# One PSUM pool, three column chunks by k half, and x through DRAM on ScalarE's queue, in a four-layer macaron trunk

## The chip, the cores and the metric

The kernel runs on one core of a Trainium2 chip. The metric is device time in microseconds (us) for one execution, lower is better; the time before is the median of three runs. TensorE is called PE, its weight loads PEld, VectorE DVE, ScalarE ACT, GpSimd POOL, and SyncE, which here only issues DMAs, SP. A name with a q (SPq, ACTq) is an engine's instruction queue.

## The reference

Four layers, each a sandwich of two half-weighted SwiGLU blocks around a mixer, on x of 256 rows by 1024 columns in float32:

```
for i in range(4):
    x = x + 0.5 * swiglu(rms_norm(x, norm_g[i, 0]), ffn_gate[i, 0], ffn_up[i, 0], ffn_down[i, 0])
    x = x + mixer_i(rms_norm(x, norm_g[i, 1]))      # i % 3: short conv, MLA, spatial gating
    x = x + 0.5 * swiglu(rms_norm(x, norm_g[i, 2]), ffn_gate[i, 1], ffn_up[i, 1], ffn_down[i, 1])

swiglu(x, g, u, d) = (silu(x @ g) * (x @ u)) @ d          # 1024 -> 2816 -> 1024
short conv:  b, c, h = split(x @ w_in, 3);  (b * causal_conv3(c * h)) @ w_out
MLA:         16-head latent attention, a = x @ w_a (416 columns), rotary parts, causal softmax
spatial:     u, v = split(gelu(x @ w_in), 2);  (u * (w_s @ rms_norm(v) + b_s)) @ w_out
```

All products are wanted at nearly float32 precision.

## The kernel before, in words

**Streams and turns.** The 256 rows are two streams of 128 rows, t0 and t1, and each runs the same twelve blocks (FFN, mixer, FFN, four times). A Python generator per stream writes the instructions in order by hand (every engine is in `MANUAL`), one *unit* of weights at a time. Turns alternate: t1, t0, t1, t0, and t0 is ahead by four advances (`LAG`). In a turn `advance` (L976) finishes the low parts of the weights made before, lets the stream write its next unit's matmuls, counts the turn and then runs the work that was put off with `later(n, ...)` and is now due (L170). So `later(1, ...)` is written at the end of the same turn, `later(8, ...)` at the end of the seventh turn after.

**Weights.** A unit is 128 x 1024 float32 values, two k tiles of 512 columns or one of 1024. SP loads it into one of six raw buffers (L91), ACT writes a rounded high part (L104), DVE the low part, the difference (L111). Each k tile of a 512-column product is three matmuls (L291, L292, L294): high x high, high x low, low x high. Both streams use the same unit, t1 four to five turns' worth of units later; there are nine buffers. A unit is made three units ahead of t0 (`AHEAD`, four counting its own), two ahead while a stream is between two blocks (`CHAIN_AHEAD`).

**Columns by k half.** A block starts with its input in two halves of 512 columns (four k tiles each), `lhs[t][0]` and `lhs[t][1]`. `linear_pair` (L344) runs the first two 512-column chunks of a block (gate and up of an FFN, c and h of the conv, both v of the spatial block) together: first half of k for both, then second half for both. That is four units of the stream, eight turns, before the second half is read. All other chunks take all eight k tiles in turn (`linear`, L296).

**x between two blocks.** A block ends in `rows_into_x` (L315), with the columns 0 to 511 of x done first, then 512 to 1023: four units later in an FFN, two in a mixer. After each half `prepare_x` (L400) turns it for the next block. By DMA: DVE transposes 32 x 32 blocks (L409); SP writes 256 KB to DRAM at the end of that turn (L414) and reads it back rearranged with four DMAs three turns later (L418); four turns after that ACT takes it with the gain (L423), writes the high part (L245), and DVE the low part (L246). By PE: four transposes (L253) into a PSUM tile, a DVE multiply by the gain (L433), then the same split. The DMA way is used after every FFN (`n % 3 != 1`, L968), PE after every mixer.

After its last unit a stream idles for two turns of its own (four ahead of MLA) in `normed` (L446), while the other goes on.

**Queues.** SP's queue is in program order and carries the raw loads (each waits for its buffer), the FFN's own way through DRAM (L267, L271) and x's writes and reads.

**PSUM.** Six banks are one pool for accumulators, `acc()`; two are another for transposes, `trp()`.

Of the kernel before, what the change touches and what calls it, by code (L numbers as in the profile page):

```python
# [13 lines left out]
F32 = mybir.dt.float32  # L14
# [33 lines left out]
N_ACC = 6  # L48
# [11 lines left out]
C_TURN, C_WAIT = 2, 0  # L60
WARM = (4, 6)
# [61 lines left out]
def trunk(ctx: ExitStack, tc: tile.TileContext, x, positions, norm_g, ffn_gate, ffn_up, ffn_down,  # L123
# [214 lines left out]
    def plan_pair(w0, w1, c0, c1, width, n_kt):  # L338
# [5 lines left out]
    def linear_pair(t, a, width, n_kt, first_done):  # L344
# [55 lines left out]
    def prepare_x(t, h, i, which, by_dma):  # L400
# [4 lines left out]
        if not by_dma:  # L405
            later(X_TURN, lambda: turn_by_pe(t, h, g))
            return
# [45 lines left out]
    def plan_ffn(i, j):  # L453
        for n, (c, w) in enumerate(FF_CHUNKS):
            if n == 0:
                plan_pair(ffn_gate[i, j], ffn_up[i, j], c, c, w, NK)
            else:
                W.add(ffn_gate[i, j], c, w, NK, UNIT // w)
                W.add(ffn_up[i, j], c, w, NK, UNIT // w)
        plan_rows(ffn_down[i, j], DFF // P, DOWN_TAIL)  # L460

    def ffn(t, i, j, _, then):
        a, r = yield from normed(t, IDLE_FIRST if i + j == 0 else (IDLE_DMA, IDLE_PE)[j])
        hs = []
        sg = [None]

        def gate_done(ps, w):
            sg[0] = slot([P, w])
            nc.scalar.activation(sg[0], ps[:, :w], AF.Silu, scale=r)  # L469

        for n, (c, w) in enumerate(FF_CHUNKS):
            if n == 0:
                up = yield from linear_pair(t, a, w, NK, lambda ps: gate_done(ps, w))
            else:
                gate = yield from linear(t, a, w, NK)
                gate_done(gate, w)
                yield
                up = yield from linear(t, a, w, NK)
            if n % 2 == 0:
                k0 = 0  # L480
                nk = sum(w for _, w in FF_CHUNKS[n : n + 2]) // P
                z = big([P, 4, nk, 32])
            h = slot([P, w])
            nc.vector.scalar_tensor_tensor(out=h, in0=up[:, :w], scalar=r, in1=sg[0], op0=ALU.mult, op1=ALU.mult)  # L484
            nc.vector.transpose(z[:, :, k0 : k0 + w // P].rearrange("p j k b -> p k j b"),  # L485
                                h.rearrange("p (k j b) -> p k j b", j=4, b=32))
            k0 += w // P
            if k0 == nk:
                turned(z, nk, hs)
            yield  # L490
# [3 lines left out]
    def plan_conv(ia):  # L494
        for j in range(2):
            if j == 0:
# [517 lines left out]
```

## Time and profile before

| | |
|---|---|
| median of 3 runs | 1893.94 us (1893.45 to 1894.00) |
| the profiled execution | 1896.66 us, its span 1894.9 us |
| mean granted TensorE clock | 0.994 |
| PE busy | 1851.4 us, 98% of the span, 8542 matmuls |
| DVE, ACT, POOL busy | 59%, 48%, 6% |
| DMA | 397 MB, 210 GB/s on average |

Busy shares are averages over the whole span. A matmul's listed duration contains the fill of the pipeline, so that consecutive matmuls overlap; the step from one start to the next tells what one costs. In brackets at the end of a timeline row stands how long the engine was idle before it and what ended that.

### The profile page before, as it was taken

To read this page: it belongs to the slowest core of one execution; us is meant where nothing else is said; L and a number is where in the kernel's file an instruction comes from. 1 tells how busy PE (TensorE), PEld (TensorE's weight loads), DVE (VectorE), ACT (ScalarE), POOL (GpSimd) and SP (SyncE) were. 2 spreads that over 40 slices of the span, in tenths; PEclk is the share of its full clock that TensorE was granted. 3 is DMA by queue.
4 is the path that set the end of the run, shared out by engine and by line. 5 is a ranking of instruction groups with operands and counts; after the bars stand their busy time and mean duration, and the time that the engine had idled before them with its cause. 6 is when DMAs were issued, how large, how long until landed. Compare 5 with 4: busy or idle time off the path is not lost.

```text
span 1894.9 us, 23349 instructions
## 1 busy us (share of the span) xinstructions
PE 1851.4 (98%) x8542; PEld 1512.8 (80%) x8542; DVE 1118.0 (59%) x1357; ACT 908.4 (48%) x1276; POOL 114.7 (6%) x222
## 2 busy tenths in 40 slices
PE   9999999999999969999989999999999999999999
PEld 7888788888788858888868887888887888788887
DVE  6565676564556466665556555666645664676563
ACT  5443554443544376544445445454445444545442
POOL 1000100000511031000010001000000000000000
PEclk9999999999999989999999999999999999999999
DMA  7776656786778640577757775567866776656782
GB/s 259 243 238 217 200 183 193 235 246 209 221 224 250 199 132 24 177 236 237 239 174 258 237 243 176 179 189 234 253 208 217 235 244 210 200 188 194 239 259 87
DMA packets 220563, 397.12 MB, mean 210 GB/s; under 512 B 16646, under 2 KB 74144, under 8 KB 220448
## 3 DMA queue, kind: packets, MB, share of 16 engines
q1 hardware_dynamic: 219440, 393.94, 66.0%
q0 software_dynamic: 608, 1.11, 0.3%
q8 instruction: 67, 1.10, 0.2%
q10 hardware_dynamic: 400, 0.57, 0.1%
q14 instruction: 48, 0.39, 0.1%
HBM read 364.10 MB, written 31.46 MB: 209 GB/s over the span
## 4 chain that ended last, share of the span: by engine, by line
PE 88%; DMA 4%; ACT 3%; DVE 3%; SPq 1%; issue 1%; ACTq 0%; DVEq 0%
PE acc L294 28%; PE acc L291 28%; PE acc L292 28%; DMA s<-xturn 3%; PE tr L253 2%; DVE wlo L111 1%; ACT s L423 1%; SPq L418 1%; ACT s L245 1%; DVE s L246 1%; DMA xturn<-s 1%; PE acc L919 1%; PE acc L892 1%; DVE x L394 0%; ACT whi L104 0%
## 5 line engine op out<-in xcount | busy, mean ns | idle before, releaser
L291 PE MATMUL acc<-whi,s 128*128 128x512 f32 (+1 forms) x2664 | 1029.8, 387 | 20.2 <-ACT s L245 19.3
L292 PE MATMUL acc<-wlo,s 128*128 128x512 f32 (+1 forms) x2664 | 1022.2, 384 | 1.5 <-DVE wlo L111 1.5
L294 PE MATMUL acc<-whi,s 128*128 128x512 f32 (+1 forms) x2664 | 982.0, 384 | 7.4 <-DVE s L246 7.3
L111 DVE TENSOR_TENSOR wlo<-raw,whi 128x1024 fp32r<-128x1024 f32 (+1 forms) x634 | 748.0, 1213 | 143.8 <-ACT whi L104 143.4
L104 ACT ACTIVATE whi<-raw 128x1024 fp32r<-128x1024 f32 (+1 forms) x634 | 635.7, 1048 | 158.0 <-PE acc L294 140.1
L291 PEld LDWEIGHTS acc<-whi,s 128*128 128x128 f32 x2664 | 502.6, 189 | 129.5 <-ACT s L245 26.1
L294 PEld LDWEIGHTS acc<-whi,s 128*128 128x128 f32 x2664 | 502.4, 189 | 119.1 <-DVE s L246 14.2
L292 PEld LDWEIGHTS acc<-wlo,s 128*128 128x128 f32 x2664 | 502.9, 189 | 105.0 <-DVE wlo L111 2.1
L469 ACT ACTIVATE s<-acc,rstd 128x512 f32<-128x512 f32 (+1 forms) x96 | 62.7, 654 | 460.7 <-PE acc L294 454.7
L484 DVE SCALAR_TENSOR_TENSOR s<-acc,rstd,s 128x512 f32<-128x512 f32 (+1 forms) x96 | 67.7, 705 | 207.4 <-PE acc L294 207.1
L278 DVE TENSOR_TENSOR s<-big,s 128x512 fp32r<-128x512 f32 x96 | 61.8, 644 | 128.8 <-ACT s L277 128.8
L246 DVE TENSOR_TENSOR s<-s,s 128x512 fp32r<-128x512 f32 (+1 forms) x58 | 39.6, 683 | 114.7 <-ACT s L245 114.7
L383 POOL TENSOR_TENSOR total<-ss,ss 128x1 f32<-128x1 f32 x26 | 14.1, 542 | 1449.5 <-ACT s L375 1449.5
L423 ACT ACTIVATE s<-s,columns 128x128 f32<-128x128 f32 x112 | 35.8, 390 | 94.0 <-DMA s<-xturn 94.0
L394 DVE SCALAR_TENSOR_TENSOR x<-acc,x 128x512 f32<-128x512 f32 x32 | 22.0, 689 | 98.8 <-PE acc L294 98.8
L375 ACT ACTIVATE s<-x 128x512 bf16<-128x512 f32 x48 | 30.0, 625 | 86.6 <-DVE x L394 50.1
L277 ACT ACTIVATE s<-big 128x512 fp32r<-128x512 f32 x96 | 56.2, 586 | 26.6 <-DMA big<-turn 26.6
L485 DVE STREAM_TRANSPOSE big<-s 128x512 f32<-128x512 f32 (+1 forms) x96 | 64.1, 668 | 3.3
L245 ACT ACTIVATE s<-s 128x512 fp32r<-128x512 f32 (+1 forms) x58 | 36.4, 627 | 46.7 <-DVE s L433 21.4
L253 PE MATMUL tr<-ident,s 128*128 128x128 f32 (+1 forms) x222 | 33.8, 282 | 7.6 <-ACT s L864 2.6
L253 PEld LDWEIGHTS tr<-ident,s 128*128 128x128 f32 (+1 forms) x222 | 26.4, 140 | 15.1 <-ACT s L864 4.4
L520 DVE SCALAR_TENSOR_TENSOR s<-s,columns,s 128x128 f32<-128x128 f32 x64 | 22.5, 352 | 2.3
(124 smaller groups left out, 432.2 us busy)
## 6 DMA issues: line engine op xcount, KB each, us to landing
raw<-in_ffn_gate_dram SPq DMA_DIRECT2D x176, 512.0 KB, 4.6
raw<-in_ffn_up_dram SPq DMA_DIRECT2D x176, 512.0 KB, 5.0
raw<-in_ffn_down_dram SPq DMA_DIRECT2D x176, 512.0 KB, 4.9
raw<-in_conv_w_in_dram SPq DMA_DIRECT2D x48, 512.0 KB, 4.4
turn<-big SPq DMA_DIRECT2D x32, 512.0 KB, 3.7
big<-turn SPq DMA_DIRECT2D x128, 128.0 KB, 4.7
raw<-in_conv_w_out_dram SPq DMA_DIRECT2D x16, 512.0 KB, 4.8
raw<-in_sg_w_in_dram SPq DMA_DIRECT2D x16, 512.0 KB, 4.6
```

Source lines behind the costliest of these rows:

```text
L104: nc.scalar.activation(hi, src, AF.Copy)
L111: self.nc.vector.tensor_tensor(out=lo, in0=src, in1=hi.bitcast(F32), op=ALU.subtract)
L246: nc.vector.tensor_tensor(out=lo, in0=src, in1=hi.bitcast(F32), op=ALU.subtract)
L253: nc.tensor.transpose(tr[: part.shape[-1], n, :], part, ident)
L277: nc.scalar.activation(hi.rearrange("p k (i b) -> p k i b", b=32), src, AF.Copy)
L278: nc.vector.tensor_tensor(out=lo.rearrange("p k (i b) -> p k i b", b=32), in0=src, in1=hi.bitcast(F32).rearrange("p k (i b) -> p k i b", b ...
L291: nc.tensor.matmul(ps, lhsT=ah[:, k, :], rhs=wh[:, wk, c], start=first, stop=False)
L292: nc.tensor.matmul(ps, lhsT=ah[:, k, :], rhs=wl[:, wk, c], start=False, stop=False)
L294: nc.tensor.matmul(ps, lhsT=al[:, k, :], rhs=wh[:, wk, c], start=False, stop=last)
L469: nc.scalar.activation(sg[0], ps[:, :w], AF.Silu, scale=r)
L484: nc.vector.scalar_tensor_tensor(out=h, in0=up[:, :w], scalar=r, in1=sg[0], op0=ALU.mult, op1=ALU.mult)
L485: nc.vector.transpose(z[:, :, k0 : k0 + w // P].rearrange("p j k b -> p k j b"), h.rearrange("p (k j b) -> p k j b", j=4, b=32))
```

## The change

PSUM becomes one pool of eight banks, `banks`, for both kinds of tile. `plan_pair` and `linear_pair` become `plan_group` and `linear_group`, which take any number of chunks, each with a function to call when its sum is complete; three chunks go by k half at the start of an FFN (gate 0, up 0, gate 1), of the conv (c, h, b of the first 512 columns) and of the spatial block (both v, first u). The rest of those blocks is rewritten in the same order of chunks. In the spatial block the product of the first u with its mix is put off by four turns (`U_WAIT`). The write of x to DRAM and its four reads go to ACT's queue. And which half goes by DMA is chosen per half: after an FFN both, but ahead of MLA only the first (the second by PE); after a mixer the second by DMA (before, both by PE).

```diff
+U_WAIT = (4, 0)
...
-    ps_acc = ctx.enter_context(tc.tile_pool(name="ps_acc", bufs=N_ACC, space=PSUM))
-    ps_tr = ctx.enter_context(tc.tile_pool(name="ps_tr", bufs=8 - N_ACC, space=PSUM))
+    banks = ctx.enter_context(tc.tile_pool(name="banks", bufs=8, space=PSUM))
...
-        return ps_acc.tile([P, 512], F32, tag="acc", name=name("acc"))
+        return banks.tile([P, 512], F32, tag="bank", name=name("acc"))
...
-        return ps_tr.tile([P, 4, P], F32, tag="tr", name=name("tr"))
+        return banks.tile([P, 4, P], F32, tag="bank", name=name("tr"))
...
+    def plan_group(parts, width, n_kt):
         for k in range(0, n_kt, n_kt // 2):
-            W.add(w0, c0, width, k + n_kt // 2, UNIT // width, k)
-            W.add(w1, c1, width, k + n_kt // 2, UNIT // width, k)
+            for w, c0 in parts:
+                W.add(w, c0, width, k + n_kt // 2, UNIT // width, k)
...
+    def linear_group(t, a, width, n_kt, done):
-        ps = [acc(), acc()]
+        ps = [acc() for _ in done]
         for k0 in range(0, n_kt, n_kt // 2):
-            for n in range(2):
+            for n in range(len(done)):
                 k = k0
                 while k < k0 + n_kt // 2:
                     w = unit(t)
                     for j in range(w[2]):
                         products([ps[n][:, :width]], a[(k + j) // 4], (k + j) % 4, w, j, [slice(0, width)], k + j == 0, k + j == n_kt - 1)
                     k += w[2]
-                    if k == n_kt and n == 0:
-                        first_done(ps[0])
-                    if k < n_kt or n == 0:
-                        yield
-        return ps[1]
+                    if k == n_kt:
+                        done[n](ps[n])
+                    yield
...
-    def prepare_x(t, h, i, which, by_dma):
+    def prepare_x(t, h, i, which, halves_by_dma):
...
-        if not by_dma:
+        if not halves_by_dma[h]:
             later(X_TURN, lambda: turn_by_pe(t, h, g))
             return
...
         def write():
-            nc.sync.dma_start(out=d.rearrange("i a j k b -> (i a) j k b"), in_=z)
+            nc.scalar.dma_start(out=d.rearrange("i a j k b -> (i a) j k b"), in_=z)
         def read():
             for j in range(4):
-                nc.sync.dma_start(out=y[32 * j : 32 * j + 32], in_=d[:, :, j].rearrange("i a k b -> a i k b"))
+                nc.scalar.dma_start(out=y[32 * j : 32 * j + 32], in_=d[:, :, j].rearrange("i a k b -> a i k b"))
...
     def plan_ffn(i, j):
+        gate, up = ffn_gate[i, j], ffn_up[i, j]
+        plan_group([(gate, 0), (up, 0), (gate, 512)], 512, NK)
+        W.add(up, 512, 512, NK, 2)
...
+        yield from linear_group(t, a, 512, NK, [lambda ps: gate_done(0, ps), lambda ps: up_done(0, ps), lambda ps: gate_done(1, ps)])
         for n, (c, w) in enumerate(FF_CHUNKS):
+            if n > 1:
+                gate_done(n, (yield from linear(t, a, w, NK)))
                 yield
+            if n > 0:
+                up_done(n, (yield from linear(t, a, w, NK)))
+                yield
...
+        yield from linear_group(t, a, 512, NK, [lambda ps, f=f: f(0, ps) for f in (c_done, h_done, b_done)])
+        for f in (c_done, h_done, b_done):
+            f(1, (yield from linear(t, a, 512, NK)))
             yield
...
+            later(U_WAIT[j], lambda: u_mixed(j))
...
+        yield from linear_group(t, a, 512, NK, [v_done, v_done, lambda ps: u_done(0, ps)])
...
-                then = (next_i, 2 * next_j, n % 3 != 1) if next_kind == "ffn" else (next_i, 1, True)
+                if next_kind == "ffn":
+                    then = (next_i, 2 * next_j, (n % 3 == 2, True))
+                else:
+                    then = (next_i, 1, (True, next_kind != "mla"))
```

## Rows read from the trace of the kernel before

**Rows 1.** The page, busy time of the engines (share of the span) xinstructions.

```profile
PE 1851.4 (98%) x8542; PEld 1512.8 (80%) x8542; DVE 1118.0 (59%) x1357; ACT 908.4 (48%) x1276; POOL 114.7 (6%) x222
```

**Rows 2.** Waits of PE: who waited for whom: us in total, times, longest us.

```profile
PE acc L291 <- ACT s L245: 19.3, 11, 7.1
PE acc L294 <- DVE s L246: 7.3, 6, 1.2
PE tr L253 <- ACT s L864: 2.6, 2, 2.1
```

**Rows 3.** Timeline of PE at the first FFN's end, and one later row.

```profile
202.98 0.39 PE L294 MATMUL acc<-whi,s 128*128 128x512 f32 x1
204.57 0.50 PE L291 MATMUL acc<-whi,s 128*128 128x512 f32 x1 [1.20 <-ACT s L245]
...
208.35 0.50 PE L294 MATMUL acc<-whi,s 128*128 128x512 f32 x1 [1.21 <-DVE s L246]
208.69 0.39 PE L291 MATMUL acc<-whi,s 128*128 128x512 f32 x1
...
1616.32 0.50 PE L291 MATMUL acc<-whi,s 128*128 128x512 f32 x1 [0.37 <-ACT s L245]
```

**Rows 4.** Timeline of PE at the start of t1's second half in FFN five.

```profile
989.96 0.80 PE L291 MATMUL acc<-whi,s 128*128 128x512 f32 x1 [2.80 <-ACT s L245]
...
993.48 0.40 PE L294 MATMUL acc<-whi,s 128*128 128x512 f32 x1
```

**Rows 5.** Timeline of PE at the start of the MLA block.

```profile
677.75 0.71 PE L291 MATMUL acc<-whi,s 128*128 128x416 f32 x1 [7.08 <-ACT s L245]
...
683.04 0.35 PE L291 MATMUL acc<-whi,s 128*128 128x416 f32 x1
...
685.49 0.46 PE L291 MATMUL acc<-whi,s 128*128 128x416 f32 x1 [0.26 <-ACT s L245]
```

**Rows 6.** Windows: length, busy of PE, PEld, DVE, ACT, POOL, PEclk, DMA share, GB/s.

```profile
677.50:683.00 5.50, 5.25 (x15) 4.68 (x16) 3.18 (x4) 4.00 (x7) 0.94 (x3) 0.52 0.30 97
990.00:994.00 4.00, 4.00 (x11) 3.17 (x12) 3.96 (x5) 2.75 (x3) 1.01 (x3) 0.57 0.72 229
```

**Rows 7.** Timeline of ACT at the first FFN's end.

```profile
192.00 1.31 ACT L423 ACTIVATE s<-s,columns 128x128 f32<-128x128 f32 x4 [6.56 <-DMA s<-xturn]
...
202.58 1.28 ACT L423 ACTIVATE s<-s,columns 128x128 f32<-128x128 f32 x4 [4.53 <-DMA s<-xturn]
```

**Rows 8.** Timeline of SP's queue there; merged rows run to the last issue's end.

```profile
192.36 4.06 SPq L414 DMA_DIRECT2D xturn<-s  x2
...
197.66 3.97 SPq L418 DMA_DIRECT2D s<-xturn  x8
```

**Rows 9.** One line each: issues of x's reads (ns min/median/max), their landing.

```profile
L418 SPq DMA_DIRECT2D s<-xturn x112: 302/423/1170, 185.3 to 1624.2; - x112
...
DMA to landing us min/median/max: 1.8/3.4/6.7
```

**Rows 10.** The same for x's writes.

```profile
L414 SPq DMA_DIRECT2D xturn<-s x28: 337/345/345, 182.6 to 1619.5; - x28
...
DMA to landing us min/median/max: 2.0/2.1/5.4
```

**Rows 11.** The page, DMA issues on ACT's queue: xcount, KB, us to landing.

```profile
s<-in_norm_g_dram ACTq DMA_DIRECT2D x1, 48.0 KB, 3.4
```

**Rows 12.** Timeline of PE around the four transposes of one half of x.

```profile
283.92 0.60 PE L253 MATMUL tr<-ident,x 128*128 128x128 f32 x4
...
284.59 0.39 PE L292 MATMUL acc<-wlo,s 128*128 128x512 f32 x1
284.82 0.40 PE L294 MATMUL acc<-whi,s 128*128 128x512 f32 x1
```

**Rows 13.** Timeline of DVE (first) and PE (second) after the second block boundary.

```profile
490.82 3.50 DVE L111 TENSOR_TENSOR wlo<-raw,whi 128x1024 fp32r<-128x1024 f32 x3 [0.41 <-ACT whi L104]
...
493.13 0.40 PE L292 MATMUL acc<-wlo,s 128*128 128x512 f32 x1
```

More of the change, by code (lines that the diff above doesn't have):

```diff
@@ L47 @@
 N_DRAM = 4
-N_ACC = 6
 AHEAD = 4
@@ L453, in plan_ffn @@
     def plan_ffn(i, j):
[L454 to L459, printed above, removed]
+        gate, up = ffn_gate[i, j], ffn_up[i, j]
+        plan_group([(gate, 0), (up, 0), (gate, 512)], 512, NK)
+        W.add(up, 512, 512, NK, 2)
+        for c, w in FF_CHUNKS[2:]:
+            for m in (gate, up):
+                W.add(m, c, w, NK, UNIT // w)
         plan_rows(ffn_down[i, j], DFF // P, DOWN_TAIL)
@@ L464, in ffn @@
         hs = []
[L465 to L469, printed above, removed]
-        for n, (c, w) in enumerate(FF_CHUNKS):
[L472 to L476, printed above, removed]
-                yield
[L478 to L490, printed above, removed]
+        sg = [None] * len(FF_CHUNKS)
@@ new lines, in ffn, with gate_done, up_done @@
+        z = []
+        def gate_done(n, ps):
+            w = FF_CHUNKS[n][1]
+            sg[n] = slot([P, w])
+            nc.scalar.activation(sg[n], ps[:, :w], AF.Silu, scale=r)
+        def up_done(n, ps):
+            w = FF_CHUNKS[n][1]
+            nk = sum(w for _, w in FF_CHUNKS[n - n % 2 : n - n % 2 + 2]) // P
+            if n % 2 == 0:
+                z[:] = [big([P, 4, nk, 32]), 0]
+            h = slot([P, w])
+            nc.vector.scalar_tensor_tensor(out=h, in0=ps[:, :w], scalar=r, in1=sg[n], op0=ALU.mult, op1=ALU.mult)
+            k0 = z[1]
+            nc.vector.transpose(z[0][:, :, k0 : k0 + w // P].rearrange("p j k b -> p k j b"),
+                                h.rearrange("p (k j b) -> p k j b", j=4, b=32))
+            z[1] += w // P
+            if z[1] == nk:
+                turned(z[0], nk, hs)
@@ L500, in plan_conv @@
+        for part in (1, 2, 0):
+            W.add(conv_w_in[ia], part * D + 512, 512, NK, 2)
         plan_rows(conv_w_out[ia], NK, OUT_TAIL)
@@ L590, in v_done @@
             sums.append(square_sum(vv))
-        v_done((yield from linear_pair(t, a, 512, NK, v_done)))
-        yield
-        rv = factor(sums)
+            if len(vs) == 2:
+                rv.append(factor(sums))
+                for j in range(2):
+                    later(3 + j, lambda j=j: normal(j))
+        rv = []
         mixed = [None] * 2
@@ L614, in gated, with u_done, u_mixed @@
             ms[j] = lhs_of(m, 4)
-        for j in range(2):
-            later(3 + j, lambda j=j: normal(j))
-        for j in range(2):
-            u = yield from linear(t, a, 512, NK)
-            us = slot([P, 512])
-            nc.scalar.activation(us, u, AF.Gelu_apprx_tanh, scale=r)
-            m = slot([P, 512])
-            nc.vector.tensor_tensor(out=m, in0=us, in1=mixed[j].rearrange("p k n -> p (k n)"), op=ALU.mult)
-            later(2, lambda j=j, m=m: gated(j, m))
-            yield
+        us = [None] * 2
+        def u_done(j, ps):
+            us[j] = slot([P, 512])
+            nc.scalar.activation(us[j], ps, AF.Gelu_apprx_tanh, scale=r)
+            later(U_WAIT[j], lambda: u_mixed(j))
+        def u_mixed(j):
+            m = slot([P, 512])
+            nc.vector.tensor_tensor(out=m, in0=us[j], in1=mixed[j].rearrange("p k n -> p (k n)"), op=ALU.mult)
+            later(2, lambda: gated(j, m))
+        yield from linear_group(t, a, 512, NK, [v_done, v_done, lambda ps: u_done(0, ps)])
+        u_done(1, (yield from linear(t, a, 512, NK)))
+        yield
         yield from rows_into_x(t, lambda k: ms[k // 4], NK, OUT_TAIL, 1.0, then)
```

40 lines of the change are left out of this document (14 added, 26 removed).

## The prediction, on record before the changed kernel was seen

> **What bounds the kernel now.** I read the page's busy shares first. The reader is to see that PE is the bound engine almost everywhere: 1851.4 of 1894.9 us, while ACT and DVE have 48% and 59% [rows 1]. Then the step between matmul starts: in an undisturbed stretch it is 0.23 us for 128x512 (284.59 to 284.82, [rows 12]), and nothing in this change alters the number or the form of those matmuls. So only time in which PE stands, runs at the lower clock level, or does transposes can be won. The view of PE's waits says how much there is to win and who is late: 19.3 us on ACT's L245 in 11 places and 7.3 us on DVE's L246 in 6 [rows 2]. L245 and L246 split x into high and low parts: PE waits for the normed input of the next block, at block boundaries after an FFN, and hardly anywhere else.
>
> The timeline of one such boundary shows two gaps [rows 3]: 1.20 us before t1's first unit (the high part of t1's first half is late) and 1.21 us before t0's fifth unit (the low part of t0's second half is late). From 202.98 to 208.69 there are ten starts, which at 0.23 us would take 2.3 us; they took 5.71. So the boundary costs 3.4 us, of which 2.4 is listed as idle and 1.0 lies in slow restarts. There are six boundaries of that kind (three FFN to FFN, three FFN to a mixer other than MLA), from 204.57 to 1616.32. Beside them stand two larger holes: 2.80 us in the fifth FFN before t1's second half [rows 4], and 7.08 us in MLA before t0's second half [rows 5].
>
> Why is x late? ACT, which takes it from DRAM, sits idle 6.56 and 4.53 us for the DMA [rows 7]. SP's queue shows the cause: t1's first half was ready to be written at 192.3 and was (192.36), but its reads were issued only at 197.66, because SP, in order, first held the write of t0's second half (which waits for DVE) and a raw load [rows 8]. The reads themselves then land after 3.4 us in the median, up to 6.7 [rows 9].
>
> **The change, part by part.** The sum is made against the profiled execution (span 1894.9, itself 1896.66); the median of the runs is 1893.94, and differences are carried over to it unchanged.
>
> (a) *Three chunks by k half.* The second half of x is first read after six of the stream's units instead of four. With both streams running that is four turns of six matmuls, 4 x 6 x 0.23 = 5.5 us later. It removes the second gap of all six boundaries (1.2 us, far under 5.5) and the 2.80 us hole of [rows 4]. After that hole PE also ran at a granted clock of 0.57 [rows 6], the 1.2 GHz level for most of it: from 989.96 to 993.48 eight steps took 3.52 us instead of 1.84: another 1.7 us. So 2.80 + 1.7 = 4.5 us. The first gap is not touched by this: t1's first half is needed when it was before, and it is what is late next.
>
> (b) *x on ACT's queue.* The write of t1's first half (ready at 192.3) goes out behind ACT's take of t0's first half and one squared sum, and lands 2.1 us later [rows 10], about 194.9. Its reads follow in ACT's order then, not at 197.66: four issues of 0.423 us [rows 9] end at 196.7, and with a landing time of 3.4 us the data is there at 200.1. ACT has by my count two whi of 1.05 us and the reads of t0's second half to pass before the take and reaches it at about 200.6; four copies and the split take 1.9 us, so the high part is ready near 202.5. PE would need it at 203.2, where it began to stand [rows 3]. The first gap closes with 0.7 us to spare. Together with (a) the six boundaries give back their 7.3 + 6.7 us of listed gaps (6.7 is the sum of the six waits on L245, 1.20 the first and 0.37 the last of them, [rows 3]) and 1.0 each of restarts: 14.0 + 5.9 = 19.9 us. Since the margin is thin, I leave 2 us of it in place.
>
> (c) *MLA: second half by PE.* PE stood 7.08 us before t0's second half and 0.26 before t1's [rows 5], and after the first it ran at a granted clock of 0.52 [rows 6]: 15 steps from 677.75 to 683.04 took 5.29 us where 0.19 us each (416 of 512 columns of 0.23) would make 2.85. By PE the half needs only residual, four transposes, a multiply and a split, and t0 is idle for four of its turns in between. So 7.34 + 2.4 = 9.7 us go. What is late next there is ACT, busy 4.0 of 5.5 us and more from there on; I count nothing inside MLA as won.
>
> (d) *Transposes on PE.* Four transposes and the slow restart take 284.59 - 283.92 = 0.67 us, where the one matmul in it costs 0.23: 0.44 us for a half [rows 12]. Eight halves (four mixers, two streams) leave PE, two (MLA) come: -6 x 0.44 = -2.6 us. The eight halves now by DMA after mixers are read 12 turns plus two idle ones after they are written to x, with the take due after eight; I cost that at nothing as long as the three chunks cover it. Without them it would be due as late as (a)'s.
>
> (e) *The price on ACT.* 34 halves go by DMA instead of 28. Each puts 0.345 + 4 x 0.423 = 2.04 us of issues [rows 9, 10] into ACT's queue, 69 us in all, and a wait for the write's landing in front of the reads. Behind these stand whi of the next units, then DVE's wlo, then PE. At an FFN's end four halves make 8.2 us, against 11.1 us in which ACT stood waiting for the DMA [rows 7], so on the whole it fits. But it is tight just after the boundary: the low part of t0's sixth unit is done at 492.0 (490.82 plus a third of 3.50) and is used at 493.13, 1.1 us later [rows 13], and PE will now come 3.4 us sooner while ACT comes some 2 us sooner. Bounds: nothing (the issues run in the shadow of the ACTIVATE before them) and 1.5 us at each of 11 boundaries, 16.5. I take 0.5 each, 5.5 us, nearer to the lower end because the excess over the margin is small.
>
> (f) *Eight banks in one pool.* A transpose in MLA waits for ACT's eviction of the one before the last, 2.6 us in all [rows 2], which more banks could give back; the group's accumulators, three per stream, hold six banks and leave the same two. ACT is the slow side in that stretch, so the evictions come no sooner. Bounds: 2.6 us gained, and as much lost where an accumulator now meets a transpose's bank. I take nothing. The put-off product of the first u (U_WAIT) is due four turns after that u, its transposes two turns later, and they are read ten turns after it: nothing.
>
> Sum: -19.9 + 2 - 4.5 - 9.7 - 2.6 + 5.5 = -29.2 us. 1893.94 - 29 = **1865 us**.
>
> **A rule weighed.** The trace before has one transfer on ACT's queue beside a full SP queue, 48 KB, and it took 3.4 us [rows 11], no less than the median on SP's queue. The Trainium skill ("DMA: Bandwidth & Descriptors", Issuing engines are not separate DMA queues) says that all queues end on the same 16 DMA engines and interleave, so that another issuing engine saves only the sequencer's time to issue. The trace agrees as far as that one row goes. By that rule a read would not land sooner on ACT's queue; the sum above already uses the 3.4 us of both queues and so stays at 1865, and a landing that gets worse is rival 1, 1870.
>
> **The rivals.**
>
> 1. *The reads land no sooner, or later, behind the raw loads.* If they take the longest landing seen, 6.7 us [rows 9], t1's first half is there at 203.4, its high part at 205.3, and the first gap stays. For it: rows 9 and 11. Against: most of the delay was SP's order, 192.7 to 197.66, not the landing. Price: the six first waits, 6.7 us, less the 2 already left: 1870 us.
>
> 2. *ACT becomes the late engine (slower than before).* ACT is in order. A read placed three turns after its write must wait for the landing, and whatever ACT holds up there delays whi, wlo and PE. If nothing of issue and landing hides, a half costs 2.04 + 2.1 = 4.1 us. At each of the seven boundaries after FFNs four halves, 16.5 us, stand against the 11.1 us of waiting that falls away [rows 7]: 5.4 us of PE time each, 38 us; t1's first half then comes no sooner either (6.7 us not won). -29 + 38 + 5 gives 1908 us. It decides from the point where ACT is more than 1.1 us later than now at the whi after the takes [rows 13]. For it: that margin. Against: ACT is free half of the time, and a queue wait while the engine still computes costs nothing.
>
> 3. *What is won at the boundary is lost beside it.* PE comes sooner, but the same raw loads, whi and wlo feed it; if these pace the stretch, as wlo's 1.22 us beside the takes could, only (c) and (d) remain, and an ACT cost of 1 us at 11 boundaries eats them: -9.7 - 2.6 + 11 = -1, 1893 us. Against: steps of 0.23 us right after each boundary in the trace.
>
> **How the numbers follow.** Forecast 0.65; rival 1 0.13; rival 2 0.14; rival 3 0.08. The forecast's own range is 1853 (nothing left, no price on ACT, 2.6 from banks, and some more from MLA's start) to 1880 (16.5 on ACT and 6.7 left). The range of 8 in 10 takes rival 1 whole and reaches toward rival 3: 1852 to 1890. Two runs of this kernel can't be told apart within 0.2%, 3.8 us. Faster (under 1890.2): forecast and rival 1, 0.78. Within: 0.08. Slower: 0.14.
>
> **What would show it.** Right: waits of PE on L245 and L246 fall from 26.6 us to a few; no hole before t1's second half or in the first 20 us of MLA, and a granted clock of 1.0 there; 56 transposes of x instead of 80; reads of x issued within 3 us of the write; landing about 3 us. Wrong: PE waiting for whi or wlo (L104, L111) after boundaries (rival 2); first gaps of a microsecond still there with reads landing above 5 us (rival 1); PE waiting for an eviction at a bank's first matmul (f). The prediction fails as a whole if the sum of PE's waits after the change is not below 20 us.

## The result, and the profile after

The changed kernel takes 1914.66 us in the median (1910.28 to 1916.47, 4 runs) against 1893.97 us (1893.45 to 1894.6) for the kernel before, timed in turn with it: ratio 1.0106, 95% interval 1.0087 to 1.0124. It is 21 us slower where 29 us less were forecast. The profiled execution took 1915.99 us (span 1914.3). Lines have moved by up to three: L290, L291 and L293 are the matmuls (L291, L292, L294 before), L244 and L245 the split of x, L252 the transposes, L391 the residual, L411 and L415 the write and the reads of x, L420 the take.

The page of the kernel after: span, busy time, and the chain that ended last, by engine and by line.

```profile
span 1914.3 us, 23335 instructions
PE 1861.1 (97%) x8518; PEld 1514.9 (79%) x8518; DVE 1121.0 (59%) x1357; ACT 917.8 (48%) x1300; POOL 104.7 (5%) x222
...
PE 80%; DMA 7%; ACT 6%; DVE 4%; ACTq 2%; issue 1%; DVEq 0%
PE acc L291 26%; PE acc L293 26%; PE acc L290 25%; DMA s<-xturn 4%; DMA xturn<-s 3%; DVE wlo L111 2%; ACT whi L104 2%; ACTq L415 2%; PE tr L252 1%; ACT s L372 1%; ACT s L420 1%; PE acc L927 1%; ACT s L244 1%; PE acc L900 1%; DVE x L391 1%
```

The engines have hardly more to do than in [rows 1]. What is new stands on the chain: the issues of x's reads on ACT's queue (2%). The transfers of x, reads and writes, stood on it before with 3% and 1% and have 4% and 3% now.

Waits of the kernel after (us in total, times, longest), those of PE first.

```profile
PE acc L291 <- DVE wlo L111: 17.4, 23, 0.8
PE acc L290 <- ACT whi L104: 14.1, 16, 2.0
...
PE acc L290 <- ACT s L244: 1.3, 1, 1.3
...
DVE wlo L111 <- ACT whi L104: 245.7, 173, 6.6
ACT whi L104 <- issue: 57.7, 28, 5.0
ACT whi L104 <- DMA s<-xturn: 56.2, 10, 6.6
```

Against [rows 2]: the waits for the split of x are gone (19.3 us in 11 places to 1.3 in one, and the 7.3 us on its low part wholly). In their place PE waits for whi and wlo, the split weights, 31.5 us in 39 places. And the last two rows say why whi is late: ACT itself stood 113.9 us in front of whi, while x's reads were issued and while those waited (the row with "issue" was 16.1 us in the trace of before, the other wasn't there).

ACT's timeline after: the first FFN's end, and the place behind the first mixer where the second tile's half goes out. An issue (ACTq) isn't counted as busy.

```profile
191.55 1.28 ACT L420 ACTIVATE s<-s,columns 128x128 f32<-128x128 f32 x4 [3.06 <-DMA s<-xturn]
...
195.98 5.80 ACTq L415 DMA_DIRECT2D s<-xturn  x8
201.83 2.00 ACT L104 ACTIVATE whi<-raw 128x1024 fp32r<-128x1024 f32 x2 [6.16 <-DMA s<-xturn]
203.74 1.26 ACT L420 ACTIVATE s<-s,columns 128x128 f32<-128x128 f32 x4
...
213.87 2.96 ACT L104 ACTIVATE whi<-raw 128x1024 fp32r<-128x1024 f32 x3 [3.51 <-issue]
...
304.43 0.34 ACTq L411 DMA_DIRECT2D xturn<-s  x1
304.82 1.06 ACT L104 ACTIVATE whi<-raw 128x1024 fp32r<-128x1024 f32 x1 [0.41 <-DVE s L406]
309.12 1.88 ACTq L415 DMA_DIRECT2D s<-xturn  x4
311.10 2.95 ACT L104 ACTIVATE whi<-raw 128x1024 fp32r<-128x1024 f32 x3 [5.21 <-DMA s<-xturn]
```

At 195.98 the reads of two halves come in a row and hold ACT for 5.80 us: eight issues of 0.444 us make 3.6, for the other 2.2 the queue stood (seven were out by 199.35, the eighth went at 201.48). The two whi behind them start at 201.83, and the take that was to gain from all this at 203.74; in the kernel before it began at 202.58 [rows 7]. Behind the mixer ACT is free from 305.9 on, but the reads go out only at 309.12. That is 4.7 us after their write, which took 4.7 us to land; the whi behind the reads waits 5.2 us in all.

PE's timeline after, at the same places, and in MLA.

```profile
202.94 0.50 PE L290 MATMUL acc<-whi,s 128*128 128x512 f32 x1 [1.04 <-ACT whi L104]
204.20 0.51 PE L291 MATMUL acc<-wlo,s 128*128 128x512 f32 x1 [0.76 <-DVE wlo L111]
214.98 0.50 PE L290 MATMUL acc<-whi,s 128*128 128x512 f32 x1 [0.50 <-ACT whi L104]
216.24 0.50 PE L291 MATMUL acc<-wlo,s 128*128 128x512 f32 x1 [0.76 <-DVE wlo L111]
312.20 0.50 PE L290 MATMUL acc<-whi,s 128*128 128x512 f32 x1 [1.36 <-ACT whi L104]
313.46 0.55 PE L291 MATMUL acc<-wlo,s 128*128 128x512 f32 x1 [0.76 <-DVE wlo L111]
674.05 0.66 PE L252 MATMUL tr<-ident,x 128*128 128x128 f32 x4 [1.20 <-DVE x L391]
683.50 1.11 PE L252 MATMUL tr<-ident,x 128*128 128x128 f32 x4 [3.48 <-DVE x L391]
```

Where the kernel before had two gaps at this boundary [rows 3], there are four, all on weights. The pair at 312.20 stands where the kernel before had none. The hole of 2.80 us [rows 4] closed, but one of 1.98 us on whi opened at 993.15.

The DMA issues (xcount, KB each, us from issue to landing), and a window of 10 us behind the mixer, with the columns of [rows 6].

```profile
s<-xturn ACTq DMA_DIRECT2D x136, 64.0 KB, 3.7
...
310.00:320.00 10.00, 7.88 (x26) 5.74 (x25) 6.45 (x6) 7.32 (x12) 0.00 (x0) 0.83 0.55 157
```

On ACT's queue the reads land no sooner than on SP's (3.4 us, [rows 9]). In the window PE did 26 matmuls; at 0.23 us ten us hold 43. 2.1 us of that are the two waits, and the granted clock fell to a mean of 0.83, so a part of the window ran at the 1.2 GHz level. The same waits stand behind the other three mixers (at 802, 1260 and 1736 us); there the mean granted clock was 0.83 in the window from 1732 and 1.00 in those from 798 and 1256.

### The profile page after: what moved, and what is told of

It is laid out like the page before. It is cut to its first block, busy times and chain, and to the rows that moved or that the text cites. A ratio compares the mean times of both kernels' runs of the same rounds, so it can differ in the third digit from the quotient of the medians.

```text
span 1914.3 us, 23335 instructions
## 1 busy us (share of the span) xinstructions
PE 1861.1 (97%) x8518; PEld 1514.9 (79%) x8518; DVE 1121.0 (59%) x1357; ACT 917.8 (48%) x1300; POOL 104.7 (5%) x222
## 4 chain that ended last, share of the span: by engine, by line
PE 80%; DMA 7%; ACT 6%; DVE 4%; ACTq 2%; issue 1%; DVEq 0%
PE acc L291 26%; PE acc L293 26%; PE acc L290 25%; DMA s<-xturn 4%; DMA xturn<-s 3%; DVE wlo L111 2%; ACT whi L104 2%; ACTq L415 2%; PE tr L252 1%; ACT s L372 1%; ACT s L420 1%; PE acc L927 1%; ACT s L244 1%; PE acc L900 1%; DVE x L391 1%
## 5 line engine op out<-in xcount | busy, mean ns | idle before, releaser
L290 PE MATMUL acc<-whi,s 128*128 128x512 f32 (+1 forms) x2664 | 1032.1, 387 | 15.9 <-ACT whi L104 14.1
L291 PE MATMUL acc<-wlo,s 128*128 128x512 f32 (+1 forms) x2664 | 1026.2, 385 | 17.5 <-DVE wlo L111 17.4
L293 PE MATMUL acc<-whi,s 128*128 128x512 f32 (+1 forms) x2664 | 983.5, 385 | 0.0
L290 PEld LDWEIGHTS acc<-whi,s 128*128 128x128 f32 x2664 | 504.0, 189 | 130.5 <-ACT whi L104 23.5
L291 PEld LDWEIGHTS acc<-wlo,s 128*128 128x128 f32 x2664 | 503.8, 189 | 129.2 <-DVE wlo L111 25.9
L293 PEld LDWEIGHTS acc<-whi,s 128*128 128x128 f32 x2664 | 503.2, 189 | 107.0 <-DVE s L245 2.3
L245 DVE TENSOR_TENSOR s<-s,s 128x512 fp32r<-128x512 f32 (+1 forms) x58 | 39.5, 681 | 63.6 <-ACT s L244 63.6
L391 DVE SCALAR_TENSOR_TENSOR x<-acc,x 128x512 f32<-128x512 f32 x32 | 22.0, 688 | 78.6 <-PE acc L293 78.6
L244 ACT ACTIVATE s<-s 128x512 fp32r<-128x512 f32 (+1 forms) x58 | 36.4, 627 | 41.7 <-DVE s L526 21.6
L420 ACT ACTIVATE s<-s,columns 128x128 f32<-128x128 f32 x136 | 43.2, 388 | 27.5 <-DMA s<-xturn 27.4
L252 PE MATMUL tr<-ident,s 128*128 128x128 f32 (+1 forms) x222 | 34.5, 284 | 8.1 <-DVE s L770 3.3
L252 PEld LDWEIGHTS tr<-ident,s 128*128 128x128 f32 (+1 forms) x222 | 26.7, 141 | 16.0 <-DVE s L770 5.1
L406 DVE STREAM_TRANSPOSE s<-x 128x512 f32<-128x512 f32 x34 | 24.2, 712 | 1.2
```

What stands on the lines that cost most here:

```text
L252: nc.tensor.transpose(tr[: part.shape[-1], n, :], part, ident)
L290: nc.tensor.matmul(ps, lhsT=ah[:, k, :], rhs=wh[:, wk, c], start=first, stop=False)
L291: nc.tensor.matmul(ps, lhsT=ah[:, k, :], rhs=wl[:, wk, c], start=False, stop=False)
L293: nc.tensor.matmul(ps, lhsT=al[:, k, :], rhs=wh[:, wk, c], start=False, stop=last)
L420: nc.scalar.activation(xg[:, k, :].rearrange("p (i b) -> p i b", b=32), y[:, :, k], AF.Copy, scale=g[:, k : k + 1])
```

## The experiments

All ratios are to the kernel before, timed in turn with it on the same chip; intervals are of 95%.

**The queue, undone and alone.** First x's DMAs put back on SP's queue, with the rest of the change kept:

```
-            nc.scalar.dma_start(out=d.rearrange("i a j k b -> (i a) j k b"), in_=z)
+            nc.sync.dma_start(out=d.rearrange("i a j k b -> (i a) j k b"), in_=z)
...
-                nc.scalar.dma_start(out=y[32 * j : 32 * j + 32], in_=d[:, :, j].rearrange("i a k b -> a i k b"))
+                nc.sync.dma_start(out=y[32 * j : 32 * j + 32], in_=d[:, :, j].rearrange("i a k b -> a i k b"))
```

> The whole change, but x's writes and reads back on SP's queue. Theory A (ACT's queue is the cost: x's issues and the waits in front of them hold back whi, then wlo, then PE): PE's waits on whi and wlo fall from 31.5 us to under 3, the seven holes on x of the kernel before are gone except the first gaps at the six boundaries (about 7 us and 3 us of restarts); time 1866 to 1876, faster than before. Theory B (the order of three chunks or the halves by DMA after mixers cost, whichever queue carries x): stays at 1900 or more.

1884.4 us, ratio 0.9939 (0.9922 to 0.9957). So the queue costs 30 us inside the change, and without it the change is faster, though by 10 us and not by 18 or more. In its waits of PE, and in the window behind the mixer, whi is hardly late any more (1.1 us in two places), wlo less than in after, and the split of x is late again. So the 30 us are net: in after the waits for that split were 1.3 us.

```profile
PE acc L290 <- ACT s L244: 9.0, 7, 1.8
PE acc L291 <- DVE wlo L111: 7.8, 10, 2.0
...
310.00:320.00 10.00, 10.00 (x44) 8.07 (x44) 6.81 (x8) 5.71 (x7) 0.00 (x0) 1.00 0.88 306
```

Behind the mixer the reads went out 4.5 us after their write there (first two rows), much as in after, but it was SP that stood, and ACT made four whi meanwhile (third row):

```profile
300.40 0.34 SPq L411 DMA_DIRECT2D xturn<-s  x1
304.91 1.75 SPq L415 DMA_DIRECT2D s<-xturn  x4
...
300.40 3.89 ACT L104 ACTIVATE whi<-raw 128x1024 fp32r<-128x1024 f32 x4
```

The other way round, the kernel before with nothing but those two lines changed to `nc.scalar`:

> The kernel before with one edit: x's writes and reads on ACT's queue. Theory A: slower than before, with PE waits on whi and wlo after each of the seven FFN boundaries (about 3.5 us each) on top of what is left of the waits on x: 1895 to 1910. Theory B: within 4 us of before or faster.

1914.01 us, 1.0098 (1.0083 to 1.0113): the queue alone makes the kernel before as slow as the whole change does. Theory A is right in sign, and the time lies 4 us above its range. The first gaps on the split of x are gone there too, the second ones are not (6.5 us in 6 places).

**The half behind the mixers, by PE again** (x still on ACT's queue):

```
-                    then = (next_i, 2 * next_j, (n % 3 == 2, True))
+                    then = (next_i, 2 * next_j, (n % 3 == 2, n % 3 == 2))
```

> The changed kernel, but after a mixer both halves are turned by PE again, so that 26 halves instead of 34 go by DMA. Theory A: the losses of 2.8 to 4.2 us after each of the four mixers (13.9 us in all) go, eight sets of transposes (3.5 us) come back: 1902 to 1906, still slower than before. Theory B, as far as it blames the three chunks alone: within 4 us of the changed kernel.

1911.83 us, 1.0086 (1.0069 to 1.0103). Theory A expected 9 to 13 us back; it is 3 us, and the intervals of 1.0086 and 1.0106 overlap. The waits behind the mixers are gone (8.7 us on whi and wlo in after), but the transposes return to PE, and at the other boundaries PE waits 26.3 us for whi and wlo, against 22.8 in after.

**A third queue, GpSimd's** (`nc.gpsimd` for the write and the reads):

> The whole change, with x's writes and reads on GpSimd's queue, whose engine is busy 5% of the time. Theory A: no whi is held back, x no longer waits behind raw loads either, so 1862 to 1880 if an issue there costs about what ACT's does; if its issue (0.5 us and more per DMA at the start of the trace) and landing (5 us and more) are that slow for x too, the waits on x come back: up to 1895. Theory B: 1900 or more.

1965.63 us, 1.0368 (1.0343 to 1.0393), far beyond either theory. An issue takes 548 ns there (one line of the issues, and their landing, 5.1 us). PE's waits are other ones than in after: 30.1 us for the split of x and 34.0 for wlo, with whi late only twice. So the late landing of x is a loss of its own, and this run is no test of what ACT's queue costs:

```profile
L415 POOL DMA_DIRECT2D s<-xturn x136: 548/548/582, 185.5 to 1779.3; - x136
...
DMA to landing us min/median/max: 2.1/5.1/7.6
```

**The other edits, one by one.** One pool of eight banks alone, in the kernel before:

```
-    ps_acc = ctx.enter_context(tc.tile_pool(name="ps_acc", bufs=N_ACC, space=PSUM))
-    ps_tr = ctx.enter_context(tc.tile_pool(name="ps_tr", bufs=8 - N_ACC, space=PSUM))
+    banks = ctx.enter_context(tc.tile_pool(name="banks", bufs=8, space=PSUM))
```

> The kernel before with one edit: PSUM as one pool of eight banks in place of six and two. Prediction's term (f): no change, 1893 to 1896. Rival, the shared banks make a transposition or an accumulation wait for a bank that the other kind holds longer: slower by 3 us or more, with waits of PE for the readers of the banks.

1894.69 us, 0.9993 (0.9983 to 1.0002): nothing. The three chunks and the pool, with x on SP's queue and every half turned as before:

```
-                    then = (next_i, 2 * next_j, (n % 3 == 2, True))
+                    then = (next_i, 2 * next_j, (n % 3 != 1, n % 3 != 1))
...
-                    then = (next_i, 1, (True, next_kind != "mla"))
+                    then = (next_i, 1, (True, True))
```

> The changed kernel with x on SP's queue and every half of x turned as in the kernel before (both by PE after a mixer, both by DMA elsewhere, before MLA too): so the three chunks by k half and the one pool alone. By the prediction's terms this is (a) and (f), 1894 less 4.5 and the restarts = 1886 to 1890; the other two terms, MLA's second half by PE and the six mixers' by DMA, would then be the rest of the way to 1884.4 (2 to 6 us, against the predicted 12.3). Rival, the chunks give nothing because wlo of the next unit comes late right behind the gap that they close: 1892 to 1895; then the 9.5 us between 1894 and 1884.4 are the two flags' alone.

1891.87 us, 0.9977 (0.9967 to 0.9988). The second gaps are gone; but the first gap stays (the first row; 1.20 in [rows 3], and 7.2 us over the six boundaries against 6.7), and at some boundaries a wlo is late soon behind it. The time lies between the two ranges expected:

```profile
205.41 0.50 PE L290 MATMUL acc<-whi,s 128*128 128x512 f32 x1 [1.93 <-ACT s L244]
...
494.07 0.50 PE L291 MATMUL acc<-wlo,s 128*128 128x512 f32 x1 [0.52 <-DVE wlo L111]
```

With only the second of those two edits, on SP's queue (MLA's second half by DMA, the mixers' as in the change):

> The changed kernel with x on SP's queue, with MLA's second half of x turned by DMA as in the kernel before: so without the prediction's term (c), which was 9.7 us. By that term 1894 (1884.4 and 9.7). Rival, the turn by PE only trades the wait for the take against a wait of PE for the residual (3.4 and 1.8 us in the traces of after) and then the clock: 1885 to 1889, and the rest of the 7.2 us between 1884.4 and the chunks alone is the six mixers' halves by DMA.

1885.91 us, 0.9947 (0.9930 to 0.9965), not distinguishable from 0.9939: MLA's half by PE is worth nothing measurable.

**What on ACT's queue costs.** The reads spread, one per turn, all on ACT:

```
-        later(X_READ, read)
+        for j in range(4):
+            later(X_READ + j, lambda j=j: read(j))
```

> The changed kernel, with the four reads of a half issued one per turn (turns 4 to 7) and no longer four in one turn; all still on ScalarE's queue. Theory A1, the place in the order (whi that PE wants soon stand behind eight reads in a row, 5.80 us at the first boundary): the whi get in between the reads, most of the 30 us that the queue costs inside the change come back: 1888 to 1896, and PE's waits for whi fall from 14.1 us to under 5. Theory A2, the mere sum of the issues on ScalarE (136 reads of 0.444 us and 34 writes of 0.344 us = 72 us, wherever they stand, and the stands for other transfers' landings): 1910 to 1920. Rival, the reads now land later (one turn is about 1.9 us, so the last one lands some 5 us later) and the take at turn 8 waits for them: 1910 or more, with the waits moved from whi to the take.

1891.73 us, 0.9982 (0.9973 to 0.9991): 23 of the 30 us come back with as many issues on the same queue. ACT still stands for the landing of x's write (the row), but PE hardly waits for whi any more (1.4 us); what PE waits for is the split of x (7.2 us in 7 places) and wlo (11.4 in 17):

```profile
ACT whi L104 <- DMA xturn<-s: 31.8, 17, 2.9
```

Write on ACT, reads on SP:

> The changed kernel, with the writes of x left on ScalarE's queue and the reads back on SP's. Theory A (the reads on ScalarE are what costs; a write is 34 issues of 0.344 us, 12 us in all, and mostly beside other work): 1884 to 1888, as with both on SP (1884.4), or up to 6 us better since SP no longer stands for DVE's transposes (120 us of waits at 28 writes in the kernel before), so that the weights behind it go out sooner: 1878 to 1888. Rival, the write's wait for DVE's transpose on ScalarE holds the whi behind it: over 1895.

1890.91 us, 0.9970 (0.9958 to 0.9982): some 6 us slower than with both on SP (0.9939), above theory A's 1888 and below the rival's 1895. So the reads in their place cost most, and a write alone costs a little, if anything: the two intervals only just part, and the two profiled executions have nearly the same span (1886.8 and 1886.4 us), so no trace shows where these 6 us lie.

Then ACT's time without any DMA: x on SP's queue, and idle activations behind each read.

```
                 nc.sync.dma_start(out=y[32 * j : 32 * j + 32], in_=d[:, :, j].rearrange("i a k b -> a i k b"))
+                nc.scalar.activation(busy, x_half(t, h), AF.Square)
```

> The changed kernel with x on SP's queue again (1884.4), and with 136 idle activations added on ScalarE, one behind each read: a square of 128x512 of x into a tile that nothing reads, so about 0.55 us of ScalarE each where the changed kernel has 0.444 us of a read's issue, four or eight in a row. No DMA is added or moved. Theory B (what the queue costs is ScalarE's time in front of the whi, whatever fills it): 1900 to 1915, with PE's waits for whi back (over 5 us) and the waits behind the mixers back at 312, 802, 1260 and 1736 us. Rival (it is the stands for other transfers' landings and the later landing of x's own reads, which this kernel hasn't): 1884 to 1891.

1887.41 us, 0.9949 (0.9932 to 0.9967). Theory B fell: 136 activations, 86 us of ACT, cost at most a few us. But that is a net figure too: PE's waits for whi and wlo rose from 8.9 us in 12 places to 14.2 in 25, and those for the split of x fell from 9.0 us in 7 places to 1.3 in one. Where PE was held at a weight first, x was no longer late. The ACT timeline of this run shows how far whi was held by them; the second place is the one of 213.87 in after:

```profile
195.59 5.25 ACT L417 ACTIVATE busy<-x 128x512 bf16<-128x512 f32 x8
200.75 1.99 ACT L104 ACTIVATE whi<-raw 128x1024 fp32r<-128x1024 f32 x2
...
208.64 2.60 ACT L417 ACTIVATE busy<-x 128x512 bf16<-128x512 f32 x4
211.15 2.94 ACT L104 ACTIVATE whi<-raw 128x1024 fp32r<-128x1024 f32 x3
```

These are about 1 us and 2.7 us earlier than in after. So the next run held ACT as long as after's trace shows it held, half by half:

```
+            for _ in range(((4, 4), (5, 6))[t][h] if halves_by_dma[0] else (5, 8)[t]):
+                nc.scalar.activation(busy, x_half(t, h), AF.Square)
```

> The changed kernel with x on SP's queue, with idle activations on ScalarE behind the reads (the same square of 128x512, some 0.65 us each in a row), but in number set to the time for which the trace of after shows the whi held: four or five for most halves (2.6 to 3.3 us), nine in a row where two halves' reads meet (5.9 us; 5.80 us in after), six for the fourth half of a boundary (3.9 us; 3.5 in after), eight for the second tile's half behind a mixer (5.2 us; 5.2 in after). No DMA is added or moved; four per half cost 3 us. Theory C (the whi are held by issues and, beyond these, by reads that stand for a landing; the first 2.6 us have cover, what comes beyond is lost): 1900 to 1912, and PE's waits behind the mixers (312, 802, 1260, 1736 us) are back. Rival (the cost is in the DMAs themselves, in queues that share something): under 1892, no waits behind the mixers.

1900.99 us, 1.0027 (1.0015 to 1.0040). Theory C holds for a good half: 39 activations more than the run before cost 14 us more, and PE's waits are those of after in kind and number, 25.9 us on whi and wlo against 31.5 (lines are one further down here):

```profile
PE acc L292 <- DVE wlo L111: 15.8, 23, 0.8
PE acc L291 <- ACT whi L104: 10.1, 15, 1.3
...
204.45 0.50 PE L291 MATMUL acc<-whi,s 128*128 128x512 f32 x1 [0.85 <-ACT whi L104]
...
313.07 0.50 PE L292 MATMUL acc<-wlo,s 128*128 128x512 f32 x1 [0.68 <-DVE wlo L111]
```

Of the 30 us it reproduces 16.6. Behind all four mixers PE waits again, but less than in after: at three of them only for the wlo, 0.6 to 0.7 us, where after has 2.1 to 2.3. The pages of the run with x back on SP and of this one, to be set against that of after:

```profile
PE 1848.0 (98%) x8518; PEld 1512.5 (80%) x8518; DVE 1119.1 (59%) x1357; ACT 915.0 (49%) x1300; POOL 112.0 (6%) x222
...
PE 1853.1 (97%) x8518; PEld 1510.0 (79%) x8518; DVE 1120.7 (59%) x1357; ACT 1020.4 (54%) x1475; POOL 103.2 (5%) x222
```

**Why x was late in the first place.** With x on SP's queue, the reads due one turn sooner:

```
-X_TURN, X_WRITE, X_READ, X_TAKE = 2, 1, 4, 8
+X_TURN, X_WRITE, X_READ, X_TAKE = 2, 1, 3, 8
```

> The changed kernel with x on SP's queue, its reads due one turn sooner (turn 3 in place of 4), so that the first half's reads stand before the second half's write in SP's order. By the same reasoning as for the second halves by PE: the first half lands some 3 us sooner, PE's waits for the first half's split (9.0 us in 7 places) fall under 3 us: 1874 to 1882. Rival, SP now stands at the reads for the write's landing (2 to 2.5 us) with the weights behind it, and these come late in their place: 1884 to 1892.

1871.42 us, 0.9868 (0.9844 to 0.9891), below the whole forecast of that run. The take of t1's first half starts at 200.62; with turn 4 on SP it was 203.44. First the SP timeline, then two takes, of this run:

```profile
184.29 1.75 SPq L415 DMA_DIRECT2D s<-xturn  x4
...
191.94 2.27 SPq L411 DMA_DIRECT2D xturn<-s  x2
194.97 0.38 SPq L91 DMA_DIRECT2D raw<-in_conv_w_in_dram  x1
195.54 4.08 SPq L415 DMA_DIRECT2D s<-xturn  x8
...
188.69 1.30 ACT L420 ACTIVATE s<-s,columns 128x128 f32<-128x128 f32 x4 [3.65 <-DMA s<-xturn]
...
200.62 1.28 ACT L420 ACTIVATE s<-s,columns 128x128 f32<-128x128 f32 x4 [4.87 <-DMA s<-xturn]
```

The reads go out at 195.54, not at 197.66 [rows 8]. They still stand behind the second write and a raw load, so the expectation had the order wrong. What moved is the half before: the reads of t0's first half (184.29) went out behind one raw load instead of two, and ACT took that half at 188.69, not at 192.62 as with turn 4. DVE, in order, had stood 1.79 us for that half's split before the transposition that the second write waits for; now it didn't. The two writes were out at 194.21, not at 197.03, and the reads behind them gained about as much. (Of each of these leads 0.9 us is older: the run was that far ahead before t0's first half was written.)

Second halves by PE at the FFN boundaries as well (x on SP's queue, reads at turn 4):

```
-                    then = (next_i, 2 * next_j, (n % 3 == 2, True))
+                    then = (next_i, 2 * next_j, (n % 3 == 2, n % 3 == 1))
...
-                    then = (next_i, 1, (True, next_kind != "mla"))
+                    then = (next_i, 1, (True, False))
```

> The changed kernel with x on SP's queue, with the second half of x turned by PE at the conv, spatial and second-FFN-to-FFN boundaries too (only the first half goes through DRAM there; behind a mixer it stays first by PE, second by DMA). If PE's first gaps come from reads that stand behind the other half's write on SP (the second write at 196.7 us waits for DVE, the reads of the first half go out from 198.3 us): the first half lands some 3 us sooner, the gaps of 0.5 to 1.8 us at six boundaries go, and PE pays 2 x 4 transposes of 0.11 us at each: 1874 to 1884. Rival, PE's turn waits for the residual of the second half as at MLA (3.4 us): 1888 to 1900.

1901.57 us, 1.0026 (1.0014 to 1.0038): its rival was right in kind, and the time is just above its range. PE, in order, stands for the residual at each boundary:

```profile
PE tr L252 <- DVE x L391: 28.6, 14, 3.1
```

The kernel before with the one constant, 3 for 4:

> The kernel before with one constant changed: x's reads due at turn 3 in place of 4, everything else, SP's queue too, as it was. If the place of the reads behind the other half's write on SP is what made the first half late (the first gaps, 18.1 us of waits for the split in [rows 2] and its like): these waits fall under 6 us, and the time is 1876 to 1884. Rival (the gain of the 1871.42 us run needs the three chunks): 1890 or more.

1883.54 us, 0.9937 (0.9922 to 0.9952). The time is in the expected range. The waits for the split's high part shrink from 19.3 us [rows 2] to 8.4, all of them in MLA or before t1's second half in FFN five, and none is left at the six boundaries; the second gaps stay, six of 1.2 us:

```profile
PE acc L291 <- ACT s L245: 8.4, 5, 4.3
PE acc L294 <- DVE s L246: 7.3, 6, 1.2
```

And the change on SP's queue with the reads at turn 2:

> The changed kernel with x on SP's queue and the reads due at turn 2, one more turn sooner than in the 1871.42 us run. If the landing still sets the time of the first half there: 1862 to 1869. If it doesn't any more (PE's waits for the first half's split were down to 1.9 us), and SP now stands some 2 us longer for the write's landing: 1870 to 1880. I take the second.

1865.92 us, 0.9850 (0.9836 to 0.9865), the fastest run here; I had taken 1870 to 1880, and the other range, 1862 to 1869, was right. Here t1's reads do go out in front of the second write (194.56 and 196.41). PE waits 5.4 us for wlo and 1.3 us for the split.

## Why the prediction was wrong

**The step that failed is (e), the price on ACT**, "I take 0.5 each, 5.5 us, nearer to the lower end because the excess over the margin is small". It measured 30 us (1914.66 against 1884.4; ratios 1.0106 and 0.9939), nearly twice the upper bound of 16.5, and that is net of 7.7 us of waits for the split of x that fell away with it. PE waits 31.5 us for whi and wlo where it waited 8.9. Three things were wrong in the step.

First, the balance "four halves make 8.2 us, against 11.1 us in which ACT stood waiting" compares sums, and ACT is in order. The 11.1 us lay in front of the takes; the issues went in front of whi. Two whi start right behind the second squared sum in the run with x on SP's queue (196.67). In after they start 6.16 us behind it, at 201.83, and PE stood for them until 202.94. Step (b) had even listed these two whi among what ACT must pass before the take, and reckoned only when x would be ready, not when the whi would.

Second, an issue was priced at its duration. 0.345 us for a write was right and 0.423 for a read near the 0.444 measured; the queue also stood: 2.2 of 5.80 us at the first FFN's end, 3.2 us (305.9 to 309.12) behind the mixer, and ACT stands with it. (b) mentioned the wait for the write's landing and (e) left it out of the 8.2 us. The spread reads' waits name that landing 17 times, and behind the mixer the stand ends with it. What the eighth read at the boundary stood for, the profile doesn't show.

Third, the cost isn't in proportion to the sum of the holds; it sets in where a margin ends. At the first FFN's end the same two whi were held for 5.1 us behind the squared sum (136 activations), 5.7 (175) and 6.2 (after); PE waited for them not at all, 0.85 and 1.04 us, and for the wlo made from them 0.77, 0.76 and 0.76. So whi's margin there is about 5 us, by my estimate from these three rows, and the 1.1 us that (e) took from another boundary [rows 13] is not the margin that decided. Beyond it PE waits twice, and at some places goes on at the lower level of the clock (0.83 in the window behind the first mixer).

So rival 2, ACT in order, then whi, then wlo, then PE, was the mechanism; it was given 0.14. That its 1908 us came near 1914.66 is in part luck, since its price sets the same sums against each other (16.5 us against 11.1).

Not settled: the idle activations reproduce 16.6 of 30 us. Between the profiled executions of that run and of after, 13.3 us of span apart, PE's busy time for the same 8518 matmuls differs by 8.0 us (1853.1 and 1861.1) and its idle time by 5.3. So the larger part of what is missing is not waits but PE working more slowly; the mean granted clock was 0.992 and 0.990. Why after has more of that than the run with the activations, no run separates.

**(b), x on ACT's queue.** The diagnosis was half right. x was late because its reads went out late: one turn sooner on SP is worth 12 us in the kernel before (0.9937). But the cure wasn't a new queue. The write, the raw load and the second write in SP's order, to which I gave the blame, stayed in the run with turn 3, and the reads passed the second write only at turn 2; the due turn of the reads was what could be moved. The waits for the split are gone in after, as forecast, but not because x came sooner: the take that was to start at about 200.6 started at 203.74, later than before, and PE, held at the weights, came to it later still. By the Trainium skill ("DMA: Bandwidth & Descriptors", Issuing engines are not separate DMA queues) another engine's queue gains only the sequencer's time. The trace agrees as far as the landing goes: 3.7 us on ACT's queue and 3.2 us on SP's in the run with x put back.

**(a), three chunks.** The gaps it named went, all six second ones and the hole. Its own terms are 7.3 and 4.5 us; with the pool it measured 4.4 (0.9977). As the text said the first gap was late next, and a wlo of 0.5 us followed at some boundaries; so part of the gain was only moved. With the first gap out of the way (turn 3) the rest of the change is worth 13 us over the kernel before with turn 3 (0.9868 against 0.9937). That holds (d)'s gain too, 5.7 us where it was measured, so some 7 us are left for (a) by that difference; no run has the chunks alone at turn 3. (a) was over-sized.

**(c), MLA's second half by PE: 9.7 us predicted, nothing measured** (0.9939 against 0.9947). The gap for the take (7.08 us before, 6.23 on SP's queue with this half by DMA) turned into two waits for the residual, 1.20 and 3.48 us in after, with PE standing in order at the transposes. The slow stretch behind it, which (c) counted as won, stayed in good part: the granted clock was 0.50 from 684 to 689 us in after and 0.66 from 679 to 684 on SP's queue, against 0.53 from 675 to 681 with the half by DMA. "What is late next there is ACT" named the wrong engine.

**(d), transposes.** Eight halves behind the mixers by DMA: 5.7 us (0.9977 to 0.9947) against 8 x 0.44 = 3.5. Right in sign, and in size as far as these intervals tell. "I cost that at nothing", the cover for those halves, held on SP's queue; on ACT's it didn't, since their reads stood in front of whi: the waits at 312.20 and three more places like it.

**(f), one pool:** nothing, as predicted (0.9993).

The sum forecast, 1865, is what the change gives without its queue and with the reads two turns sooner (1865.92). That the numbers meet is chance: (c) gave nothing, (a) less than its term, and the due turn of the reads, which no term had, gave the rest.

## What to carry to other kernels

Price a DMA issued from a computing engine by what stands behind it in that engine's order: its issue, every landing that it waits for, and the first instruction behind it that the bound engine needs, against that instruction's margin at that place. When a transfer is late, first look whether its issue was due late in its own queue; one turn was worth 12 us here, and another queue cost 20 to 30. A gain at one gap should be counted only after asking what is late 0.5 us behind it.

## What the runs showed of the hardware

- A read's issue takes 0.42 to 0.44 us on SP's and ACT's queues and 0.55 us on GpSimd's, where the landing was also longest (5.1 us against 3.2 on SP's and 3.7 on ACT's) and the kernel 3.7% slower. The landings are those of the changed kernel with x on the three queues.
- A queue whose head stands for a landing stops its engine's arithmetic: ACT's activations waited up to 6.6 us behind reads that were being issued or stood. On SP's queue a stand of 4.2 us (300.74 to 304.91) let ACT make four whi.
- 86 us of added activations on an engine that is busy for 48% of the time cost 3 us net, with the waits for x falling as those for weights rose; 25 us more, at chosen places, cost 14.
